# Conditioning rows at 0.7, 1.1, 1.1, 1.1 and 0.7 per block in five mixer projections, in place of 0.94 in all five

## Chip, cores and metric

The kernel runs on one core of a Trainium2 chip. The metric is the device time of one execution in microseconds, as the median of several runs. Before the change it is 2046.04 us (three runs, 2045.04 to 2049.21).

## The reference

One layer of a flow-matching trunk is applied to 128 context tokens and 256 latent tokens of width 2048. Both groups share the weights; each has its own conditioning vector, from which a matrix w_mod (2048 x 12288) makes six modulation vectors: sh1, sc1, g1 for the mixer and sh2, sc2, g2 for the feed-forward part.

```python
def _layer(x, mod, grid, s_ret0, c0, n0, m0, lp):
    sh1, sc1, g1, sh2, sc2, g2 = jnp.split(mod, 6, axis=-1)
    h = _ln(x) * (1.0 + sc1) + sh1
    mix, states = _mixer(h, grid, s_ret0, c0, n0, m0, w_in, b_gate, conv_qk, ret_theta,
                         gn_ret, gn_mlstm, w_out)
    x = _ln(ALPHA * x + g1 * mix) * ln1_g + ln1_b
    h = _ln(x) * (1.0 + sc2) + sh2
    x = _ln(ALPHA * x + g2 * _ffn(h, grid, w_up, conv_ff, w_down)) * ln2_g + ln2_b
    return x, states
# mod = silu(c) @ w_mod + b_mod, for the context's and the latents' vector
```

The mixer projects h with w_in (2048 x 8208), runs four heads of retention and four of mLSTM in both directions over the tokens, normalises each head, multiplies it by a gate and projects the result with w_out (2048 x 2048). The states of the context are outputs too.

## The kernel before

All 384 tokens are kept as 16 tiles of 128 features (kt = 0 to 15). Matrix products run in float32 split in two parts: ScalarE copies a weight tile to hi (L117), VectorE, and for one tile in six GpSimd, makes lo = raw - hi (L118), and TensorE adds three products, ah x hi, al x hi and ah x lo (L182 to L184 for products whose output has features on the partitions, tile psa; L190 to L192 for those with tokens on the partitions, tiles psb and pso).

**Mixer projections.** Heads are taken in a fixed order, four of retention and then four of mLSTM. The first two are projected in an earlier stage together with the first modulation vectors. A loop over i = 2 to 7 projects the other six. i = 2 and 3 are the last two of retention, i = 4 to 7 are the four of mLSTM, so the fourth projection is i=3 and the last is i=7. Each has 16 blocks, called steps here: 4 for q and 4 for k (psa, four kt in one weight tile, 24 matmuls) and 8 for v and gate (psb, two kt in one tile, 18 matmuls).

**What runs beside a step.** After each step, `beside()` gives one step to three generators: `mods2` (conditioning rows), `gating` (the gates of mLSTM) and `behind` (the attention of an earlier head). A Stepper collects its rate as credit and takes one item for each whole unit:

```python
        def step(self):
            self.credit += self.rate
            while self.gen is not None and self.credit >= 1.0:
                self.credit -= 1.0
                if next(self.gen, self) is self:
                    self.gen = None
```

Beside projection i runs the attention of head i-2; beside i=7 run those of heads 5 and 6, at rate 1.55. The attention of head 7, called attention(7), runs beside the first seven blocks of w_out, at rate 1.75, and is finished before the eighth.

**Conditioning rows.** `mod_vector` computes g1, sh2 and the first half of sc2 on VectorE, in five macc blocks of 16 rows. A row loads a tile mraw of 128 x 1024 of w_mod (512 KB, three buffers, loads two rows ahead, on SyncE's queue) and makes two VectorE instructions on macc, one for each conditioning vector (L283 for the first row of a block, L286 for the others). After 16 rows eight small matmuls with a matrix of ones sum macc over the partitions (L293, tile modr); VectorE adds the bias (L295) and GpSimd's queue writes the vector to DRAM (modrow). macc has one buffer, so the next block's first row can't start before this reduction has read the last one. The reduction of a block and the first row of the next are one item of the generator: the 17th, 33rd, 49th and 65th item, and the 81st ends it.

**Order.** The framework orders each engine's instructions before the program runs: an engine takes the instruction that stands first in the program among those that its own timing model holds ready. Work that stands later in the program can so be taken early where an engine would else be idle. On the chip each engine keeps that order.

**After the loop.** Attention(5) and (6) fill the last tiles of the mixer's output. The w_out product for the first 512 columns (tile pso) runs over kt 0 to 11, 14 and 15 in seven blocks, each followed by a step of `mods2` and of attention(7); kt 12 and 13 come from attention(7) and make the eighth block. The rest of w_out, the feed-forward part and the norms follow.

Of the kernel before, what the change touches and what calls it, by code (L numbers as in the profile page):

```python
# [82 lines left out]
def hybrid_step(ctx, tc, ca, cb, x_prompt, x_sample, state_ret, state_c, state_n, state_m, c, c_ctx,  # L83
# [51 lines left out]
    def rows_bcast(dst, src_row, n):  # L135
        nc.gpsimd.dma_start(out=dst, in_=src_row.to_broadcast([P, n]))
# [133 lines left out]
    def mod_vector(part, psp, mp, raws, js=range(2)):  # L270

        for j in js:
            col = part * D + j * 1024
            acc = mp.tile([P, 2, 1024], F32, tag="macc", name="macc", bufs=1)
            bt = mp.tile([P, 512], F32, tag="mbt", name="mbt", bufs=1)
            for hf in range(2):
                nc.gpsimd.dma_start(out=bt[64 * hf:64 * hf + 64, :],
                                    in_=b_mod[:, col + hf * 512:col + (hf + 1) * 512].to_broadcast([64, 512]))
            for kt in range(KT):
                raw = next(raws)  # L280
                for v in range(2):
                    if kt == 0:
                        nc.vector.tensor_scalar(out=acc[:, v, :], in0=raw, scalar1=ct[:, kt, v:v + 1],  # L283
                                                scalar2=None, op0=ALU.mult)
                    else:
                        nc.vector.scalar_tensor_tensor(out=acc[:, v, :], in0=raw, scalar=ct[:, kt, v:v + 1],  # L286
                                                       in1=acc[:, v, :], op0=ALU.mult, op1=ALU.add)
                yield
            ps = psp.tile([P, 512], F32, tag="ps", name="modr")
            for hf in range(2):  # L290
                for v in range(2):
                    g = 2 * hf + v
                    nc.tensor.matmul(ps[32 * g:32 * g + 32, :], lhsT=ones, rhs=acc[:, v, hf * 512:(hf + 1) * 512],  # L293
                                     start=True, stop=True)
            nc.vector.tensor_tensor(bt, ps, bt, op=ALU.add)  # L295
            for hf in range(2):
                for v in range(2):
                    g = 2 * hf + v
                    nc.gpsimd.dma_start(out=modrow[part, v:v + 1, j * 1024 + hf * 512:j * 1024 + (hf + 1) * 512],
                                        in_=bt[32 * g:32 * g + 1, :])  # L300
# [18 lines left out]
    def chain(*gens):  # L319
        for g in gens:  # L320
            yield from g
# [192 lines left out]
    with p1:  # L514
# [72 lines left out]
        def gates():  # L587
# [49 lines left out]
            for n, src in enumerate((ga, gem)):  # L637
                for d in range(2):
                    for tt in range(NT):
# [8 lines left out]
        mods2 = Stepper(chain(mod_vector(2, pat, mp, raws2), mod_vector(3, pat, mp, raws2),  # L648
                              mod_vector(4, pat, mp, raws2, range(NV))), 0.9)
# [257 lines left out]
        def attention(i):  # L907
            return heads[i][1](heads[i][2], *got[i])

        def new_acts(*kts):  # L910
            for kt in kts:
                new_act(kt, mixt[kt])

        for i in range(2, 8):
            mods2.rate = 0.0 if i == 2 else 0.94
            gating.rate = 0.6 if i == 3 else 0.0
            if i == 6:
                gating.finish()
                gn_m.append(tab.tile([P, 1024], F32, tag="gn", name="gnm"))
                rows_bcast(gn_m[0], gn_mlstm.rearrange("a h v -> a (h v)"), 1024)  # L920
            last = i == 7
            behind[:] = [Stepper(chain(*[attention(j) for j in ((5, 6) if last else (i - 2,))]), 1.55 if last else 1.0)]
            got.append(heads[i][0](heads[i][2], [lambda j=j: new_acts(2 * j, 2 * j + 1) for j in range(5)] if last else ()))
            behind.pop().finish()
        new_acts(10, 11, 14, 15)
        wo = w_out[0]
        pso = [pmm.tile([P, 512], F32, tag="ps", name="pso") for _ in range(NT)]
        attn = Stepper(attention(7), 1.75)
        attn.step()
        for k0 in (0, 2, 4, 6, 8, 10, 14):  # L930
            part_b(pso, weights_b(wo, k0, 2, (0,)), 2, k0, 0, 13)
# [55 lines left out]
    with ExitStack() as p2:  # L987
# [130 lines left out]
        for kt in range(KT):  # L1118
            if kt % 4 == 0:
                for ug in range(2):  # L1120
# [4 lines left out]
                    i = kt // 2 + ug  # L1125
# [238 lines left out]
```

## Time and profile before

| what | value |
|---|---|
| median of three runs | 2046.04 us (2045.04 to 2049.21) |
| profiled execution | 2043.59 us, of which the program's span is 2041.8 us |
| TensorE (PE) busy | 1982.6 us, 97% of the span |
| VectorE (DVE) busy | 1244.4 us, 61% |
| projections i = 2 to 7 | 228.5 to 733.5 us from the span's start |
| first 512 columns of w_out up to the eighth block | 733.5 to 799 us |

PE is TensorE's matmuls, PEld its weight loads, DVE VectorE, ACT ScalarE, POOL GpSimd, SP SyncE. Lines such as L286 are lines of the kernel. In the rows of instructions, "out<-in" names tiles, "x32" counts instructions, and a bracket gives the idle time of the engine before the first of them and what ended it. Busy matmuls are modelled from their starts, so PE can be called busy where it is not at its peak.

### The profile page before, as it was taken

To read this page: it belongs to the slowest core of one execution; us is meant where nothing else is said; L and a number is where in the kernel's file an instruction comes from. 1 tells how busy PE (TensorE), PEld (TensorE's weight loads), DVE (VectorE), ACT (ScalarE), POOL (GpSimd) and SP (SyncE) were. 2 spreads that over 40 slices of the span, in tenths; PEclk is the share of its full clock that TensorE was granted. 3 is DMA by queue.
4 is the path that set the end of the run, shared out by engine and by line. 5 is a ranking of instruction groups with operands and counts; after the bars stand their busy time and mean duration, and the time that the engine had idled before them with its cause. 6 is when DMAs were issued, how large, how long until landed. Compare 5 with 4: busy or idle time off the path is not lost.

```text
span 2041.8 us, 26592 instructions
## 1 busy us (share of the span) xinstructions
PE 1982.6 (97%) x10333; PEld 1747.4 (86%) x10333; DVE 1244.4 (61%) x1805; ACT 707.9 (35%) x1082; POOL 237.8 (12%) x233
## 2 busy tenths in 40 slices
PE   6899998999999998999999999999999999999997
PEld 4677888798898886678999889999889998999976
DVE  4555795487969894476964333449534445544478
ACT  4223334333343543236333333333222332333341
POOL 0001332231222222024000000000000000000003
PEclk9899999999999999998999999999999999999999
DMA  9895679587768765834764334447434444534342
GB/s 342 253 310 184 183 193 155 118 221 206 231 211 208 186 203 178 310 102 117 236 198 126 124 124 124 125 124 245 142 124 124 124 124 165 165 114 135 121 142 88
DMA packets 260638, 352.32 MB, mean 173 GB/s; under 512 B 16143, under 2 KB 200784, under 8 KB 259360
## 3 DMA queue, kind: packets, MB, share of 16 engines
q1 hardware_dynamic: 256240, 340.08, 55.6%
q0 software_dynamic: 4272, 10.54, 1.5%
q8 instruction: 81, 1.33, 0.3%
q14 instruction: 45, 0.37, 0.1%
HBM read 343.16 MB, written 7.41 MB: 172 GB/s over the span
## 4 chain that ended last, share of the span: by engine, by line
PE 84%; DVE 7%; issue 3%; DMA 3%; POOL 1%; SPq 1%; ACT 1%; DVEq 0%; POOLq 0%; ACTq 0%
PE psu L182 12%; PE psu L184 12%; PE psu L183 12%; PE psd L192 5%; PE psd L191 5%; PE psd L190 5%; PE psa L182 4%; PE psa L184 4%; PE psa L183 4%; PE psb L190 3%; PE psb L191 3%; PE psb L192 3%; DVE macc L286 3%; PE modps L255 2%; DMA mraw<-in_w_mod 2%
## 5 line engine op out<-in xcount | busy, mean ns | idle before, releaser
L118 DVE TENSOR_TENSOR lo<-raw,hi 128x1024 fp32r<-128x1024 f32 (+4 forms) x446 | 485.1, 1095 | 535.3 <-ACT hi L117 534.6
L117 ACT CAST hi<-raw 128x1024 fp32r<-128x1024 f32 (+4 forms) x476 | 438.0, 930 | 966.5 <-PE psu L183 358.5
L183 PE MATMUL psu<-al,hi 128*128 128x384 f32 (+1 forms) x1336 | 450.6, 338 | 0.0
L182 PE MATMUL psu<-ah,hi 128*128 128x384 f32 (+1 forms) x1336 | 448.9, 338 | 0.0
L184 PE MATMUL psu<-ah,lo 128*128 128x384 f32 (+1 forms) x1336 | 447.1, 338 | 0.0
L286 DVE SCALAR_TENSOR_TENSOR macc<-mraw,ct,macc 128x1024 f32<-128x1024 f32 x210 | 287.9, 1397 | 15.3 <-DMA mraw<-in_w_mod 15.1
L182 PEld LDWEIGHTS psu<-ah,hi 128*128 128x128 f32 x1336 | 249.5, 188 | 1.8 <-issue 0.8
L183 PEld LDWEIGHTS psu<-al,hi 128*128 128x128 f32 x1336 | 250.7, 188 | 0.1
L184 PEld LDWEIGHTS psu<-ah,lo 128*128 128x128 f32 x1336 | 250.5, 188 | 0.1
L191 PE MATMUL psd<-lo,fah 128*128 128x512 f32 (+1 forms) x496 | 194.9, 393 | 2.4 <-DVE lo L118 2.4
L192 PE MATMUL psd<-hi,fal 128*128 128x512 f32 (+1 forms) x496 | 196.6, 396 | 0.0
L190 PE MATMUL psd<-hi,fah 128*128 128x512 f32 (+1 forms) x496 | 189.7, 391 | 0.0
L184 PE MATMUL psa<-ah,lo 128*128 128x384 f32 x512 | 175.3, 344 | 7.0 <-DVE lo L118 6.9
L182 PE MATMUL psa<-ah,hi 128*128 128x384 f32 x512 | 179.5, 355 | 1.7 <-ACT hi L117 1.7
L183 PE MATMUL psa<-al,hi 128*128 128x384 f32 x512 | 175.3, 343 | 0.0
L191 PE MATMUL psb<-lo,ah 128*128 128x512 f32 x384 | 153.8, 401 | 0.5 <-DVE lo L118 0.5
L192 PE MATMUL psb<-hi,al 128*128 128x512 f32 x384 | 152.5, 397 | 0.0
L190 PE MATMUL psb<-hi,ah 128*128 128x512 f32 x384 | 149.9, 405 | 0.7 <-ACT hi L117 0.7
L191 PEld LDWEIGHTS psd<-lo,fah 128*128 128x128 f32 x496 | 93.1, 188 | 27.3 <-DVE lo L118 4.0
L182 PEld LDWEIGHTS psa<-ah,hi 128*128 128x128 f32 x512 | 96.6, 190 | 17.7 <-issue 11.6
L190 PEld LDWEIGHTS psd<-hi,fah 128*128 128x128 f32 x496 | 93.1, 188 | 21.7 <-ACT hi L117 0.2
L192 PEld LDWEIGHTS psd<-hi,fal 128*128 128x128 f32 x496 | 93.1, 188 | 21.3
(329 smaller groups left out, 2343.2 us busy)
## 6 DMA issues: line engine op xcount, KB each, us to landing
raw<-in_w_up SPq DMA_DIRECT2D x168, 512.0 KB, 3.8
mraw<-in_w_mod SPq DMA_DIRECT2D x112, 512.0 KB, 4.9
raw<-in_w_down SPq DMA_DIRECT2D x84, 512.0 KB, 3.6
raw<-in_w_in SPq DMA_DIRECT2D x128, 256.0 KB, 4.6
raw<-in_w_in SPq DMA_DIRECT2D x52, 512.0 KB, 7.1
wm<-in_w_mod SPq DMA_DIRECT2D x20, 1024.0 KB, 8.9
raw<-in_w_out SPq DMA_DIRECT2D x32, 512.0 KB, 4.7
wm<-in_w_mod SPq DMA_DIRECT2D x16, 768.0 KB, 6.1
```

The lines of the kernel that those rows point to most:

```text
L117: mark["hi"] = nc.scalar.copy(dst_hi, src).ins
L118: mark["lo"] = (eng or nc.vector).tensor_tensor(out=dst_lo, in0=src, in1=dst_hi.bitcast(F32), op=ALU.subtract).ins
L182: nc.tensor.matmul(ps, lhsT=hi[:, s], rhs=ah, start=start, stop=False)
L183: nc.tensor.matmul(ps, lhsT=hi[:, s], rhs=al, start=False, stop=False)
L184: nc.tensor.matmul(ps, lhsT=lo[:, s], rhs=ah, start=False, stop=stop)
L190: nc.tensor.matmul(ps, lhsT=ah[:, t], rhs=hi[:, s], start=start, stop=False)
L191: nc.tensor.matmul(ps, lhsT=ah[:, t], rhs=lo[:, s], start=False, stop=False)
L192: mark["mm"] = nc.tensor.matmul(ps, lhsT=al[:, t], rhs=hi[:, s], start=False, stop=stop).ins
L255: nc.tensor.matmul(ps[32 * g:32 * g + 32, :w], lhsT=ct[:, kt, :], rhs=raw[:, kk * w:(kk + 1) * w], start=kt < 4, stop=kt >= 12)
L286: nc.vector.scalar_tensor_tensor(out=acc[:, v, :], in0=raw, scalar=ct[:, kt, v:v + 1], in1=acc[:, v, :], op0=ALU.mult, op1=ALU.add)
```

## The change

In the loop over projections the rate of `mods2` is 0.7 for i=3 and i=7 and 1.1 for i = 4, 5 and 6, in place of 0.94 for all five. For i=2 it stays 0. After the loop the rate is set to 0.94, so that the steps beside w_out have the rate that they had. Nothing else is changed: rows, blocks, reductions, buffers and queues are the same.

```diff
         for i in range(2, 8):
-            mods2.rate = 0.0 if i == 2 else 0.94
+            mods2.rate = (0.0, 0.7, 1.1, 1.1, 1.1, 0.7)[i - 2]
             gating.rate = 0.6 if i == 3 else 0.0
...
         pso = [pmm.tile([P, 512], F32, tag="ps", name="pso") for _ in range(NT)]
         attn = Stepper(attention(7), 1.75)
+        mods2.rate = 0.94
         attn.step()
         for k0 in (0, 2, 4, 6, 8, 10, 14):
             part_b(pso, weights_b(wo, k0, 2, (0,)), 2, k0, 0, 13)
             mods2.step()
```

## The prediction

> **What bounds the kernel now.** The page comes first. In it TensorE (PE) is busy almost throughout, so a change to VectorE (DVE) work can pay only where PE waits for it.
>
> ```profile
> span 2041.8 us, 26592 instructions
> PE 1982.6 (97%) x10333; PEld 1747.4 (86%) x10333; DVE 1244.4 (61%) x1805; ACT 707.9 (35%) x1082; POOL 237.8 (12%) x233
> L286 DVE SCALAR_TENSOR_TENSOR macc<-mraw,ct,macc 128x1024 f32<-128x1024 f32 x210 | 287.9, 1397 | 15.3 <-DMA mraw<-in_w_mod 15.1
> ```
>
> A conditioning row is two DVE instructions on macc, 2 x 1.397 = 2.8 us by that group. Second view: busy time by stage, cut where the projection loop goes from one i to the next (i=2, 3, 5, 6 and 7 shown). The columns are the bounds, the length, busy time with instruction counts, the granted clock and the DMA.
>
> ```profile
> core 0: us, PE busy (x) PEld busy (x) DVE busy (x) ACT busy (x) POOL busy (x), PEclk, DMA share, GB/s
> 228.50:313.00 84.50, 80.45 (x393) 71.51 (x392) 78.87 (x96) 27.93 (x51) 34.28 (x28) 0.98 0.75 205
> 313.00:403.60 90.60, 85.65 (x418) 72.82 (x417) 49.09 (x78) 32.96 (x57) 19.89 (x19) 0.98 0.70 131
> 483.70:563.00 79.30, 79.30 (x400) 70.42 (x399) 65.64 (x77) 27.86 (x40) 18.08 (x18) 1.00 0.67 210
> 563.00:644.00 81.00, 81.00 (x400) 70.52 (x399) 63.61 (x103) 32.63 (x55) 17.29 (x17) 1.00 0.71 203
> 644.00:733.50 89.50, 88.15 (x434) 74.99 (x433) 80.00 (x126) 43.87 (x81) 24.52 (x20) 1.00 0.75 197
> ```
>
> Both stages that lose rows are some 10 us longer than their neighbours, but i=7 mostly because it carries two heads' attention (434 matmuls against 400). PE idles 5.0 us in i=3 and 1.4 us in i=7. Third view: the waits of PE in those two stages, and what DVE did before the first.
>
> ```profile
> PE psa L184 <- DVE lo L118: 5.0, 1, 5.0
> PE psa L184 <- DVE lo L118: 1.3, 1, 1.3
> 312.02 4.07 DVE L286 SCALAR_TENSOR_TENSOR macc<-mraw,ct,macc 128x1024 f32<-128x1024 f32 x2 [3.27 <-DMA mraw<-in_w_mod]
> 316.01 4.10 DVE L118 TENSOR_TENSOR lo<-raw,hi 128x512 fp32r<-128x512 f32 x4
> ```
>
> The 5.0 us stand at the start of i=3: a row's data landed late, and the split that PE needed stood behind it on DVE.
>
> The larger loss lies after the projections, in the part of w_out where the last head's attention ends. Fourth view: PE from the seventh w_out step on, and two of its waits.
>
> ```profile
> 761.60:777.00 15.40, 14.08 (x64) 10.80 (x64) 10.32 (x32) 8.53 (x17) 4.61 (x4) 1.00 0.47 151
> 777.00:799.00 22.00, 15.47 (x59) 9.98 (x58) 12.13 (x41) 8.56 (x23) 3.59 (x4) 0.87 0.30 100
> 781.10 0.70 PE L794 MATMUL num<-vx,wt 128*128 128x257 f32 x2 [2.58 <-DVE wt L762]
> 796.14 1.13 PE L114 MATMUL mxp<-cst,hh 128*128 128x128 f32 x6 [3.08 <-DVE hh L713]
> ```
>
> PE is idle 1.32 + 6.53 = 7.85 us there: its w_out blocks are used up at 777, and it follows the serial chain of head attention(7). That chain starts late because the one before it ended late. Fifth view: DVE from scores to the transposed output for attention(5), (6) and (7), first all of it, then macc alone.
>
> ```profile
> 650.30:696.80 46.50, 37.83 (x73) 1.00 0.79 179
> 699.48:769.70 70.22, 69.12 (x104) 1.00 0.64 211
> 769.78:797.20 27.42, 14.57 (x49) 0.93 0.31 106
> 650.30:696.80 46.50, 15.14 (x11) 1.00 0.79 179
> 699.48:769.70 70.22, 36.30 (x26) 1.00 0.64 211
> 769.78:797.20 27.42, 0.00 (x0) 0.93 0.31 106
> ```
>
> With no macc beside it such a head takes 27.4 us, with 11 macc 46.5, with 26 macc 70.2, and there DVE is busy 98%. So attention(6) is bound by DVE, half of it by conditioning rows.
>
> **The change part by part.** It adds and removes no instruction: both versions hand out 75 rows in i=3 to 7 (16 x 0.94 x 5 = 75.2 and 16 x (0.7 + 3 x 1.1 + 0.7) = 75.2), and w_out starts from the same credit at 0.94 again. What moves is where in the program each row and each block's reduction stands. 16 rows fill one macc (a single buffer); a reduction (L293, on PE) ends a block and frees macc for the next. Engines' orders are planned from program order, with later work pulled ahead into idle time. Sixth view: macc in the stretches of blocks (x32) and the breaks between (PE x8 is the reduction that ends a break).
>
> ```profile
> 316.20:420.40 104.20, 1.07 (x8) 0.16 (x8) 0.00 (x0) 0.98 0.67 131
> 420.40:482.30 61.90, 0.00 (x0) 0.00 (x0) 43.57 (x32) 1.00 0.86 239
> 503.90:569.10 65.20, 0.00 (x0) 0.00 (x0) 42.87 (x32) 1.00 0.73 239
> 569.10:593.20 24.10, 1.06 (x8) 0.16 (x8) 0.00 (x0) 1.00 0.47 142
> 593.20:661.00 67.80, 0.00 (x0) 0.00 (x0) 44.87 (x32) 1.00 0.85 221
> 661.00:690.10 29.10, 1.06 (x8) 0.16 (x8) 0.00 (x0) 1.00 0.79 172
> 690.10:761.60 71.50, 0.00 (x0) 0.00 (x0) 45.07 (x32) 1.00 0.64 204
> ```
>
> *i=3, rate 0.94 to 0.7: nothing, 0 us.* The first break covers it: block 1 is over at 316, three microseconds into i=3, so all its rows were pulled into i=2, where the rate is 0. They stay behind all work of i=2 and the first steps of i=3 in either version, so I expect the same order and the same 5.0 us stall. Bounds: 0, and a gain of 5.0 us if row 16, which hereafter belongs to step 5 of i=4 instead of step 2, no longer gets ahead of the split.
>
> *i=4 to 6, rate 1.1: reductions move.* Counting credit, the 17th call comes at step 6 of i=4 (11.2 + 6 x 1.1) instead of step 3, the 33rd at step 4 of i=5 in both, the 49th at step 3 of i=6 (46.4 + 3.3) instead of 5, the 65th at step 2 of i=7 (64.0 + 1.4) instead of 6. A projection step is 24 psa matmuls in its first half; seventh view, psa in windows that hold 6, 3 and 2 such steps, and the reduction as it is now.
>
> ```profile
> 403.58:437.90 34.32, 26.79 (x144) 1.00 0.70 172
> 562.90:578.30 15.40, 13.35 (x73) 1.00 0.72 248
> 643.90:657.80 13.90, 9.72 (x48) 1.00 1.00 255
> 688.40:689.60 1.20, 1.06 (x8) 0.16 (x8) 1.00 0.12 44
> ```
>
> So block 2 runs from about 439 to 501 (its 61.9 us), just before block 3 begins at 503.9, which stays; block 4 runs from about 580 to 648 (67.8 us) instead of 593 to 661; block 5 may start at about 659 instead of 690. In i=5 and i=6 the rates put 16 x 0.16 = 2.6 more rows each (7.2 us) into 13.7 and 17.4 us of idle DVE (79.30 - 65.64, 81.00 - 63.61). I cost this at 0; the cover is that idle time and the splits that lie ready for PE. If it is gone, PE stalls on lo as at 313: 0 to 5.0 us for each stall, and I take 0, since block 2 to 4 each ran in a DVE that was nearly full and i=5 and 6 show PE busy to the last hundredth. The moved reductions issue their bias and modrow DMAs on POOL's queue with them; the rows' loads move on SP's queue and are issued when a macc row frees one of three mraw buffers, so they follow the blocks.
>
> *i=7, rate 0.7, and the earlier fourth reduction.* Here the gain comes from. Eighth view: DVE in the present break, and the macc of block 4 in i=7.
>
> ```profile
> 661.00:690.00 29.00, 29.00 (x155) 26.15 (x154) 20.33 (x58) 14.44 (x30) 5.05 (x7) 1.00 0.79 171
> 647.65 4.07 DVE L286 SCALAR_TENSOR_TENSOR macc<-mraw,ct,macc 128x1024 f32<-128x1024 f32 x2 [0.83 <-DMA mraw<-in_w_mod]
> 652.78 4.60 DVE L286 SCALAR_TENSOR_TENSOR macc<-mraw,ct,macc 128x1024 f32<-128x1024 f32 x2
> ```
>
> In the break DVE has 29.0 - 20.3 = 8.7 us idle that block 5 could not use and now can. Besides, 8.7 us of block 4's macc leave i=7 for i=6. After the break, attention(6) competed with 16 rows that were overdue; at 0.7 a row, fewer stand ahead of it in the program. So attention(6) should end earlier by 0 (if rows only change places with its own work) to 17.4 us; I take 8.7, the idle time alone, since the other 8.7 us fall where macc is not yet free. Attention(7), 27.4 us long, then starts at 761 and ends at 788.5 instead of 797.2, beside the last two w_out blocks. PE can take back at most the 7.85 us it idles. I take 8: the gain is -8, between 0 and -10.
>
> At 796 to 799 PE also runs at a lowered clock after the 3.08 us wait; the reduction there is the row at half speed.
>
> ```profile
> 797.20 1.94 PE L293 MATMUL modr<-macc,ones 128*32 128x512 f32 x8
> ```
>
> It takes 1.94 us against 1.06 at full clock. I leave that as it is: the wait for hh ends the chain in either version. [...]
>
> *The sum.* 0 (i=3) + 0 (i=4 to 6) - 8 (end of attention) = -8 us. The profiled execution took 2043.59 us (span 2041.8, 1.8 around it), so 2035.6 by it. It lies 2.45 us under the median of 2046.04; taken to the median, 2038.
>
> **The rivals.** First, nothing happens: the rows are low in priority already, attention(6) is slowed by its own 104 - 26 other instructions and by the splits, and ends where it did. For it: in i=3 exactly that holds. Against it: 26 macc and 36.3 us of its 70.2. It gives 2046, within 4 us.
>
> Second, slower: rows 76 to 80 still stand in w_out at 0.94, and if attention(6) ends early they fall into attention(7), which has no macc now. Its chain is serial; 10 macc ahead of its links would cost 10 x 1.4 = 14 us. It decides once more than 6 macc (8.7 / 1.4) stand there. For it: 26 macc stretched attention(6). Against it: with block 5 begun 31 us sooner, its last row, now at 761, should be done at 740 to 750. If all ten fell there and attention(6) gained half (4 us), the time is 2046 - 4 + 14 = 2056.
>
> Third, the stall of i=3 goes as well: 8 + 5 = 13 us, 2033.
>
> **How the numbers follow.** The forecast, some 5 to 11 us faster, has 0.62, the third rival 0.06, no difference 0.21, slower 0.11. A difference under 0.2% (4.1 us) is about what can't be told from no change here, the three runs alone spread over 4.2 us. Faster 0.68, same 0.21, slower 0.11. The range goes from 2033 (third rival) to 2048, which takes in half of the no-difference case; outside are the slower rival and some of the ends.
>
> **What would show it.** Right: in i=3 two macc at 312 and a PE wait of 5.0 us as before; reductions near 438, 503, 579 and 658; macc nearly without a break from 659; attention(6) over by about 760; PE idle after 761 down from 7.85 us to some 2. Wrong: reduction 4 still near 688, or PE waiting on macc for it; new PE waits on lo in i=5 to 7; macc among attention(7)'s instructions; i=3 shortened, in which case pulling ahead doesn't work as I read it.

## The result, and the profile after

The changed kernel takes 2059.81 us (median of four runs, 2058.97 to 2062.19), the kernel before 2045.54 us beside it (four runs, 2042.94 to 2049.21). The ratio is 1.0075, 95% interval 1.0063 to 1.0086: slower by 14 us, where 8 us less was forecast and 2033 to 2048 given as the range.

The page of the changed kernel, and its stages i=3, 6 and 7 and the first part of w_out (bounds, length, busy time with instruction counts by engine, granted clock, DMA share, GB/s):

```profile
span 2060.4 us, 26584 instructions
PE 1988.6 (97%) x10333; PEld 1750.3 (85%) x10333; DVE 1245.9 (60%) x1805; ACT 704.4 (34%) x1079; POOL 236.6 (11%) x233
```

```profile
core 0: us, PE busy (x) PEld busy (x) DVE busy (x) ACT busy (x) POOL busy (x), PEclk, DMA share, GB/s
313.70:404.20 90.50, 85.67 (x417) 72.92 (x416) 49.05 (x78) 32.86 (x57) 19.83 (x19) 0.98 0.70 132
564.40:649.40 85.00, 82.99 (x400) 71.67 (x400) 70.81 (x101) 32.53 (x55) 18.00 (x16) 0.98 0.78 221
649.40:739.80 90.40, 85.95 (x407) 73.24 (x406) 84.87 (x125) 36.73 (x63) 22.27 (x16) 0.96 0.77 201
739.80:770.00 30.20, 30.20 (x133) 23.54 (x132) 14.58 (x30) 16.06 (x29) 6.99 (x6) 1.00 0.34 114
770.00:796.00 26.00, 21.39 (x85) 16.57 (x84) 12.04 (x41) 8.28 (x24) 3.92 (x7) 0.87 0.25 81
796.00:818.00 22.00, 15.47 (x59) 10.27 (x59) 12.58 (x42) 8.47 (x23) 3.79 (x5) 0.84 0.31 102
```

The same work is done (PE has as many matmuls, DVE as many instructions), and i=3 is as long as it was. i=6 takes 85.0 us instead of 81.0. DVE is nearly full in i=7, and half empty from 739.8 on; PE idles in i=6 and i=7 (2.0 and 4.5 us), and again from 770 on (11.1 us to 818).

The two profiled spans lie 18.6 us apart, more than the 14.3 of the medians: the profiled execution of before is 2.0 us under its median, that of after 2.4 above. Where the 18.6 us arise is read from three marks. The loop's i=6 begins at 564.44 (before 562.87), i=7 at 649.38 (643.88), the eighth w_out block at 817.68 (799.10). From that block to the end of the span both executions take 1242.7 us (2060.4 - 817.7, 2041.8 - 799.1). So 1.6 us come ahead of i=6, 3.9 from i=6, and 13.1 from i=7 and the seven w_out blocks. PE in these two stretches, without other engines; two rows of before, then two of after:

```profile
562.87:643.88 81.01, 81.01 (x399) 1.00 0.71 203
643.88:799.10 155.22, 146.02 (x678) 0.98 0.64 182
```

```profile
564.44:649.38 84.94, 82.93 (x400) 0.98 0.78 221
649.38:817.68 168.30, 152.71 (x678) 0.94 0.56 154
```

Length less busy time is PE's idle time: 9.2 us before and 15.6 after in the long stretch, 6.4 more. The other 6.7 of the 13.1 us are busy time: the same 678 matmuls took longer at a lower granted clock (0.94 against 0.98). In i=6 it is the same: 2.0 us idle and 1.9 more busy. PE's waits there, first i=6, then the long stretch:

```profile
PE psb L191 <- DVE lo L118: 2.0, 1, 2.0
```

```profile
PE mxp L114 <- DVE hh L713: 6.1, 2, 3.1
PE psb L191 <- DVE lo L118: 3.5, 1, 3.5
```

The prediction's view of DVE from a head's scores to its transposed output, now for attention(5), (6) and (7); first all of DVE, then macc alone:

```profile
660.42:749.21 88.79, 79.89 (x119) 0.96 0.71 195
749.32:785.67 36.35, 18.99 (x53) 0.97 0.35 116
785.88:815.43 29.55, 14.64 (x49) 0.85 0.21 72
660.42:749.21 88.79, 43.26 (x32) 0.96 0.71 195
749.32:785.67 36.35, 0.00 (x0) 0.97 0.35 116
785.88:815.43 29.55, 0.00 (x0) 0.85 0.21 72
```

All 32 macc of block 5 now stand beside attention(5), which takes 88.8 us instead of 46.5. Attention(6) is quick, as forecast (36.4 instead of 70.2), but begins 50 us later and ends 16 us later than before. After 749 there is no macc left, and two serial chains follow each other on a DVE that is half idle. How a row gets between the links of a chain, and how the new stall of i=7 arises (DVE, then PE; a bracket gives the idle time before, and what ended it):

```profile
687.16 5.42 DVE L286 SCALAR_TENSOR_TENSOR macc<-mraw,ct,macc 128x1024 f32<-128x1024 f32 x2
...
693.10 1.27 DVE L286 SCALAR_TENSOR_TENSOR macc<-mraw,ct,macc 128x1024 f32<-128x1024 f32 x1
...
694.94 1.27 DVE L286 SCALAR_TENSOR_TENSOR macc<-mraw,ct,macc 128x1024 f32<-128x1024 f32 x1
696.13 1.21 DVE L118 TENSOR_TENSOR lo<-raw,hi 128x1024 fp32r<-128x1024 f32 x1
...
707.35 0.14 DVE L797 TENSOR_TENSOR dn<-dn,gcol 128x1 f32<-128x1 f32 x1
707.42 1.27 DVE L286 SCALAR_TENSOR_TENSOR macc<-mraw,ct,macc 128x1024 f32<-128x1024 f32 x1
708.62 0.15 DVE L798 RECIPROCAL dn<-dn 128x1 f32<-128x1 f32 x1
```

```profile
697.40 0.50 PE L191 MATMUL psb<-lo,ah 128*128 128x512 f32 x1 [3.53 <-DVE lo L118]
```

Two links of the normaliser, 0.14 and 0.15 us long, have a macc of 1.27 us between them. Four macc stand in the 9 us ahead of the split at 696.13 (5.42 us for two of them, where two take 2.47 at 670.47; what stands beside them is in the last section), and PE waits 3.53 us for that split, whose hi was ready at 691.1.

### The profile page after: what moved, and what is told of

Same layout as the page of the kernel before. It is cut to its first block, busy times and chain, and to the rows that moved or that the text cites. A ratio compares the mean times of both kernels' runs of the same rounds, so it can differ in the third digit from the quotient of the medians.

```text
span 2060.4 us, 26584 instructions
## 1 busy us (share of the span) xinstructions
PE 1988.6 (97%) x10333; PEld 1750.3 (85%) x10333; DVE 1245.9 (60%) x1805; ACT 704.4 (34%) x1079; POOL 236.6 (11%) x233
## 4 chain that ended last, share of the span: by engine, by line
PE 82%; DVE 8%; DMA 4%; issue 3%; SPq 1%; POOL 1%; ACT 1%; DVEq 0%; POOLq 0%; ACTq 0%
PE psu L183 11%; PE psu L184 11%; PE psu L182 11%; PE psd L192 5%; PE psd L191 5%; PE psd L190 5%; PE psa L182 3%; PE psb L191 3%; PE psb L190 3%; PE psb L192 3%; DVE macc L286 3%; PE psa L184 3%; PE psa L183 3%; DMA mraw<-in_w_mod 2%; PE pso L190 2%
```

## The experiments

Each was measured beside the kernel before; the medians of before were 2044.76, 2044.46, 2044.02 and 2043.85 us in the four groups (e1, e2, e4, e5; e3, e6, e7, e8; e9, e10; e11, e12). Edits are against the kernel before unless said otherwise.

**e1_hold: the new rates up to i=6, the fourth reduction left at step 6 of i=7.** In `beside()` (against the changed kernel):

```diff
-            mods2.step()
+            if hold[0]:
+                hold[0] -= 1
+            else:
+                mods2.step()
...
-            mods2.rate = (0.0, 0.7, 1.1, 1.1, 1.1, 0.7)[i - 2]
+            mods2.rate = (0.0, 0.7, 1.1, 1.1, 1.1, 11.2 / 11)[i - 2]
+            hold[0] = 5 if i == 7 else 0
```

> Rates as in the changed kernel up to i=6 (64 rows handed out), but in i=7 no row before step 6, then 11.2/11 a step, so that the fourth reduction stands at step 6 as before the change. Theory A (the loss comes from block 5 starting at step 2 of i=7, which takes the macc-free stretch from attention(5)): most of the loss goes, 2045 to 2051 us; attention(5) again near 46 us. Theory B (the loss comes from the four more rows in i=6, which delay attention(4) and with it the chain of the last heads by 12 us): most of the loss stays, 2054 to 2060 us.

Measured: 2052.69 us, ratio 1.0035 (1.0022 to 1.0048), 7.9 us over before. macc beside attention(5) and (6):

```profile
659.60:706.70 47.10, 3.94 (x5) 1.00 0.66 145
709.20:777.00 67.80, 37.41 (x27) 0.99 0.63 209
```

The two heads take what they took before (47.1 and 67.8 against 46.5 and 70.2). What is left is the part ahead: i=7 starts 4.6 us later (648.5 against 643.9), and attention(4) ends at 659.8 instead of 648.3. The time lies between the ranges of the two theories: each has a part. Of the 7.9 us, 4.0 arise in i=6 (563.5 to 648.5 here) and 3.3 from i=7 to the eighth block (648.5 to 807.0).

**e2_last: the reverse, the old rates up to i=6 and the fourth reduction at step 2 of i=7, then 0.7 a step.**

```diff
-            mods2.rate = 0.0 if i == 2 else 0.94
+            mods2.rate = (0.0, 0.94, 0.94, 0.94, 0.94, 0.7)[i - 2]
+            mods2.credit += 3.84 if i == 7 else 0.0
```

> Rates as before the change up to i=6 (60 rows), but in i=7 the credit is raised by 3.84 at the start and the rate is 0.7, so that the fourth reduction is handed out at step 2 as in the changed kernel. Theory A: most of the loss is there, 2052 to 2060 us, attention(5) over 70 us. Theory B: little of it, 2044 to 2051 us, since attention(4) ends as before the change, near 648.

Measured: 2059.87 us, ratio 1.0072 (1.0055 to 1.0089), 15.1 us over before. macc beside attention(5), and the reduction:

```profile
651.20:747.50 96.30, 53.60 (x37) 0.96 0.76 208
660.91 3.03 PE L293 MATMUL modr<-macc,ones 128*32 128x512 f32 x8 [2.80 <-DVE macc L286]
```

The earlier fourth reduction alone gives the whole loss. Here it even stops PE for 2.8 us: its last macc was not yet done. The two parts don't add: 7.9 + 15.1 = 23 against 14 for both together.

**e4_after_no5 and e5_before_no5: block 5's sums left out, in the changed kernel and in the kernel before.** In `mod_vector`:

```diff
             for kt in range(KT):
                 raw = next(raws)
                 for v in range(2):
+                    if part == 4 and kt > 0:
+                        continue
```

> The changed kernel with block 5's sums left out but for its first row (its loads and its reduction stay; the first half of sc2 is wrong by that). Theories A and B agree that macc beside the attention of the last heads stretches their chain; A: without it the changed kernel has almost no loss left beside the one of the kernel before with the same cut, both at 2032 to 2040 us, within 4 us of each other. B: it stays 8 to 12 us behind that kernel, since attention(4) still ends late.

> The kernel before with block 5's sums left out but for its first row. Both theories: attention(6) falls from 70 us to 30 to 45 us, PE idles less after 761 us, and the time is 2034 to 2039 us (7 to 11 us less). If the time stays at 2043 to 2047 us, macc is not what stretches the chain.

Measured: 2045.23 us (e4) and 2038.36 (e5, ratio 0.9966, 0.9954 to 0.9977). Against before of its own group the changed kernel is at +14.3, e4 at +0.5 (ratio 1.0003, 0.9994 to 1.0013), e5 at -6.4. So block 5's sums cost 6.4 us before and 13.8 after: 7.4 of the 14.3 us are a higher price for the same 30 macc. The other 6.9 (e4 less e5) are there without them, and agree with e1's 7.9. The 6.9 lie between what theory A (within 4) and theory B (8 to 12) had expected, as in e1, and e4's time is above A's 2032 to 2040.

**e3_first: rates 0.7, 1.1, 1.02, 0.94, 0.94, the fourth reduction at step 6.**

```diff
-            mods2.rate = 0.0 if i == 2 else 0.94
+            mods2.rate = (0.0, 0.7, 1.1, 1.02, 0.94, 0.94)[i - 2]
```

> Only the first two of the five rates changed for good: 0.7, 1.1, 1.02, 0.94, 0.94, so that 45.12 rows are out at the end of i=5 and all is as before from i=6 on. Theory C (only the order of macc against the attention of heads 4 to 7 counts, which is one serial chain up to the eighth w_out block): no difference that can be told, 2043 to 2048 us. Rival D (back-to-back macc blocks cost PE time wherever they stand): i=4 longer by 2 us as in the changed kernel and the rest later by that or more, 2048 to 2052 us.

Measured: 2045.19 us, ratio 1.0004 (0.9995 to 1.0013). Nothing: the change in i=3, 4 and 5 alone is free, and attention(5) to (7) are as before (46.6, 70.1 and 27.5 us). With e1, the part ahead of i=7 that costs is the 1.1 in i=6 (85.0 us long in e1 too).

**e8_thin: as before up to step 6 of i=7, then 0.35 a step, the rest at 1.78 beside w_out.** A counter set at i=7 changes the rate from step 7 on:

```diff
+                if late7[0] == 10:
+                    mods2.rate = 0.35
...
+        mods2.rate = 1.78
```

> As before the change up to step 6 of i=7, where the fourth reduction stands; then only 0.35 rows a step in i=7 and 1.78 in w_out. Theory C with rows pulled ahead into idle time: what paces the rows of a block is DVE's idle time, not the rate; attention(6) still has over 20 macc beside it and the time is 2042 to 2048 us. Rival E (a lower rate puts attention(6) ahead of the rows in the order, as I had predicted): attention(6) ends 5 us or more earlier and the time is 2036 to 2041 us.

Measured: 2044.81 us, ratio 1.0 (0.9991 to 1.0009). macc beside attention(6), with a third of the rate:

```profile
699.50:769.70 70.20, 37.04 (x26) 1.00 0.66 215
```

It is the row of before (70.22 us, 26 macc). Handing rows out more thinly did not take them from beside attention(6): they are pulled ahead from where they stand, as the rows of block 1 are at 312. Here the place of the reduction, which frees macc, set when block 5 ran, and the rate behind it did nothing.

**e6_early, e7_from2, e9_burst: macc taken out of i=7**, by rates that finish the rows about its start or earlier.

```diff
-            mods2.rate = 0.0 if i == 2 else 0.94
+            mods2.rate = (0.0, 2.0, 1.0, 1.0, 1.0, 1.0)[i - 2]        # e6
+            mods2.rate = 1.0                                           # e7, i=2 too
+            mods2.rate = 0.0 if i == 2 else 1.3                        # e9
+            mods2.credit += 16.0 if i == 3 else 0.0                    # e9
```

> Rates 0, 2.0, 1.0, 1.0, 1.0, 1.0: 32 rows are out at the end of i=3, 80 at the end of i=6, and the first reduction moves from i=4 to step 9 of i=3, where DVE has 41 us idle. Theory C: no macc beside attention(5), (6) and (7); attention(4) still has some 30 to 40; the chain ends as in the kernel before with block 5's sums left out or a little earlier, 2033 to 2040 us. Rival D: DVE is full from i=3 to i=6 without a break, PE stalls on lo there, and it is 2044 us or more.

> Rate 1.0 in all six projections, i=2 too: the first reduction moves to step 1 of i=3, and 80 rows are out at the end of i=6. Theory C: as with 2.0 in i=3, but attention(4) has fewer macc beside it, since each block starts earlier; 2031 to 2039 us; rows 1 to 16 were in i=2 anyway. Rival D: 2044 us or more, by stalls in i=2 and i=3.

> Rate 0 in i=2, 16 rows of credit at the start of i=3 and 1.3 a step from there: reductions at step 1 and 14 of i=3, 10 of i=4, 6 of i=5 and 2 of i=6, so all macc is done by about 575 us and none stands beside the attention of heads 4 to 7 but for the first part of 4. Theory A: the end of the chain is as hidden as PE's own work allows; PE gains up to 10 us there and loses 4 to 8 us by waits on lo in i=3 to i=5, where DVE is full without a break; 2036 to 2044 us. Rival D (DVE without breaks costs more than that): 2046 us or more.

Measured: 2060.38 us (e6, ratio 1.0078, 1.0064 to 1.0091), 2048.91 (e7, 1.0021, 1.0012 to 1.003) and 2055.55 (e9, 1.0061, 1.0048 to 1.0074). PE from the start of i=2 to that of i=7, before and then in e7, and in e7 from there to the eighth block:

```profile
228.52:643.88 415.36, 406.36 (x2005) 0.99 0.73 193
```

```profile
228.51:657.11 428.60, 413.61 (x2017) 0.99 0.78 212
657.10:801.80 144.70, 141.15 (x669) 0.99 0.48 121
```

The last stretch is 10.5 us shorter than before (144.7 against 155.2), but i=7 begins at 657.1 instead of 643.9. PE idles 15.0 us ahead of it against 9.0. The other two begin i=7 at 670.0 and 669.1. All three miss the gain that theory C or A had expected of them and fit rival D's times. PE's waits for splits from i=2 to i=6 in e9 (13.3 us together in e6):

```profile
PE psa L184 <- DVE lo L118: 11.3, 3, 5.0
PE psb L191 <- DVE lo L118: 4.8, 4, 2.5
```

Before, these two were 5.0 and 0.5 us. With macc earlier and closer together the splits are late more often. That it is DVE's fullness alone is not shown: the longest new wait in e9 (4.8 us, at 606.5) follows 3.54 us in which DVE waited for a row's data.

**e11_step4, e12_step8 and e10_later: the fourth reduction at step 4, 8 and 10 of i=7** (before: 6; e2: 2), nothing changed ahead of i=7.

```diff
+            mods2.credit += 1.88 if i == 7 else 0.0                    # e11
...
+            if not 6 <= n7[0] <= 7:        # e12; e10: 6 to 9. No row in these steps,
+                ...                        # then 10.34 / 9 (e10: 10.34 / 7) a step
                 mods2.step()
```

> Before's rates with 1.88 more credit at the start of i=7: the fourth reduction is the item of step 4 of i=7 instead of step 6, nothing before i=7 changes. Theory (the place of the fourth reduction splits block 5 between attention(5) and attention(6)): some 18 to 22 macc beside attention(5), which takes 62 to 72 us instead of 46.8, and some 12 beside attention(6), which takes 50 instead of 70.1; attention(6) ends within 4 us of before's 769.5 and the time is within 5 us of before's. Rival (any reduction ahead of step 6 gives what step 2 gives): attention(5) over 85 us, no macc beside attention(6), some 2058.

> Before's rates, but in i=7 the conditioning rows rest in steps 6 and 7; the fourth reduction is the item of step 8, and the rest follow at 10.34/9 a step, 0.94 again in w_out. Theory (place of the fourth reduction): attention(5) about 45 us with 4 to 8 macc, attention(6) 72 to 80 with 26 to 30 macc, the time 2 to 10 us over before's, between step 6 (0) and step 10 (+13). Rival (a smooth optimum at step 6 is not there, the two steps only shift block 5 within attention(6)): within 2 us of before's.

> As before the change, but the rows rest from step 6 to 9 of i=7, so that the fourth reduction stands at step 10 in place of 6 (rate 10.34/7 from there). Theory A (the break's place counts): attention(5) keeps its macc-free stretch, attention(6) begins without macc and gets it from about 715, attention(7) gets the last rows; the loss of 15 us at step 2 does not go on as a gain, 2041 to 2049 us. If an earlier reduction costs and a later one pays in proportion (4 steps for 15 us), it would be under 2038 us.

Measured: 2048.90 (e11, ratio 1.0026, 1.0016 to 1.0036), 2050.09 (e12, 1.0033, 1.0021 to 1.0046) and 2056.89 (e10, 1.0062, 1.0047 to 1.0078). By the step of the reduction the time over before is 15.1 at 2, 5.1 at 4, 0 at 6, 6.2 at 8 and 12.9 at 10. macc beside attention(5) and (6) in e11, then e12, then e10:

```profile
649.50:735.10 85.60, 43.83 (x33) 1.00 0.82 226
735.00:774.10 39.10, 6.08 (x5) 0.96 0.36 123
```

```profile
651.40:696.40 45.00, 8.32 (x6) 1.00 0.81 182
700.90:775.20 74.30, 39.15 (x30) 0.97 0.63 209
```

```profile
651.70:695.70 44.00, 8.51 (x5) 1.00 0.77 171
699.70:783.80 84.10, 42.89 (x32) 0.94 0.58 189
```

The later side is as thought: 26, 30 and 32 macc beside attention(6) at steps 6, 8 and 10, which takes 70, 74 and 84 us. At step 10 its last links come after the w_out blocks are used up, and PE waits once 6.7 us for a dn product; the 2041 to 2049 us that theory A had expected there were missed. On the early side my account was only half right. At step 4 nearly all of block 5 is beside attention(5) too (33 macc of 43.8 us, 85.6 us long), not split as I had expected, yet that costs 5.1 and not 15.1 us. What step 2 has besides, in e2 and in the changed kernel alike, is PE stopped within i=7 (2.8 us for macc and 2.5 us for wt in e2, 3.5 us for lo in the changed kernel), each with a lowered clock after it (0.57 at 660 to 664 and 0.75 at 696 to 700 in e2, 0.50 at 700 to 704 in the changed kernel). e11 has no such stop, and the granted clock stays at 1.00 beside attention(5). The stop near 697 in the changed kernel follows two macc that were slow (5.42 us for both, where 1.27 is usual for one), but one of 3.32 us at 750.17 in the kernel before stops nothing (PE is busy without a gap from 746 to 762). Why those stops come at step 2 and not at 4 is open; so is why the two parts of the change don't add.

No version that was run with all its sums beats the kernel before.

## Why the prediction was wrong, point by point

**i=3: right.** Two macc at the same place and the same stall (4.8 us for lo against 5.0), and the stage is as long:

```profile
312.77 3.98 DVE L286 SCALAR_TENSOR_TENSOR macc<-mraw,ct,macc 128x1024 f32<-128x1024 f32 x2 [3.24 <-DMA mraw<-in_w_mod]
```

**Where the reductions go: right.** Forecast near 438, 503, 579 and 658; they stand at 435, 504, 582 and 665. The last macc ended at 738, forecast 740 to 750.

**"i=4 to 6, rate 1.1": costed at 0, measured at 7 to 8.** e1 gives 7.9, e4 against e5 6.9, and e3 puts it on i=6. There 34 macc instead of 29 stand beside attention(4), which takes 91.9 us instead of 81.2 and ends 12 us later (660.6 against 648.3), and PE has one wait on lo of 2.0 us. The cover that I named, idle DVE, was there in sum (85.0 - 70.8 = 14.2 us) but not where it was needed: DVE stands for 3.50 us ahead of a row whose data came late, and the split that PE needs, whose hi was ready at 637.5, comes behind that row.

```profile
638.75 1.28 DVE L286 SCALAR_TENSOR_TENSOR macc<-mraw,ct,macc 128x1024 f32<-128x1024 f32 x1 [3.50 <-DMA mraw<-in_w_mod]
...
641.55 1.20 DVE L118 TENSOR_TENSOR lo<-raw,hi 128x1024 fp32r<-128x1024 f32 x1
```

It is the stall of 312 in another place (3.24 us for the data there). I had put "0 to 5.0 us for each stall" and taken 0 because PE was busy to the last hundredth. That showed that nothing was late at the old rate, not how much room there was.

**"i=7, rate 0.7, and the earlier fourth reduction": the step that decided.** It was taken at -8 and bounded from 0 to 17.4 us of gain for attention(6), with no loss; e2 alone measures +15.1. Three things in it failed.

- I counted the break from 661 to 690 as 8.7 us of idle DVE for block 5 to fill. It was also the stretch in which attention(5) had its 46.5 us: a serial chain leaves DVE idle between links while other engines do theirs, and a macc started there makes the next link wait (1.27 us of macc at 707.42, ahead of a link of 0.15). With block 5 in it, attention(5) took 88.8 us. Its length alone does not set the time, though: 85.6 us of it cost 5.1 in e11, where PE had no new stop in i=7.
- I looked for the price at attention(7), the second rival, and found no macc there. That was so (0 macc). The head that paid was the one ahead, whose chain I had just shown as the quick one.
- I took PE's idle 7.85 us as the most at stake (the sum took 8 and its bound 10, both over it). New stalls lay in i=6 and i=7, where PE had idled 0 and 1.35 us, and the 7.85 themselves grew to 11.1 (from 770 on): PE waits there for hh of attention(6) too, some 3 us.

From i=7's start to the eighth block DVE now works less, and idles 20 us more (155.2 - 130.8 = 24.4 before, 168.3 - 123.8 = 44.5 after):

```profile
643.88:799.10 155.22, 130.77 (x234) 0.98 0.64 182
```

```profile
649.38:817.68 168.30, 123.77 (x236) 0.94 0.56 154
```

The macc taken early leave DVE nothing to do while attention(6) and (7) run one after the other. Idle time was moved, not filled.

**What would have told it.** My sign of a wrong forecast, "new PE waits on lo in i=5 to 7", came true (2.0 us in i=6, 3.5 in i=7). "No difference" fell too; the slower rival gave 2056, near the measured time, by a mechanism that did not occur.

## What to carry to other kernels

Idle time of an in-order engine is not free for low-priority work where a serial chain runs through it (here attention(5) went from 46.5 to 88.8 us): count the chain's links there, and what each waits when a longer instruction stands ahead, before calling it cover. Ask too whether the added work waits for a load, since what stands behind it then waits as well (in i=6 DVE stood 3.50 us for a row's data, and PE waited 2.01 us for the split behind that row). A break set by one buffer can be what lets the chain beside it run, so cost its filling as a loss first. When bulk work can't be removed, try its place from both sides: here each two steps of moving the release of macc off step 6, either way, cost 5 to 10 us.

## What of the hardware was not expected

A short stall of PE cost about twice its length here. In i=6 of the changed kernel PE waited 2.01 us, and the matmuls behind it ran slower for a while:

```profile
642.81 0.50 PE L191 MATMUL psb<-lo,ah 128*128 128x512 f32 x1 [2.01 <-DVE lo L118]
...
643.64 0.63 PE L191 MATMUL psb<-lo,ah 128*128 128x512 f32 x1
...
644.92 1.92 PE L810 MATMUL cst_ps<-vx,kw 128*128 128x257 f32 x4
...
647.04 0.40 PE L192 MATMUL psb<-hi,al 128*128 128x512 f32 x1
```

The slow stretch begins 0.8 us after PE resumed and lasts some 3.4 us (643.64 to 647.04). The granted clock was 0.51 in it, and 1.00 from 564.44 up to it and from its end to 649.38. By these two numbers it holds some 1.7 (3.4 x 0.49) of the 1.9 us of busy time that i=6 has more than before, beside the 2.0 of the wait. After the 3.53 us wait of i=7 the granted clock was 0.50 in one window of 4 us (700 to 704), with 0.77 and 0.87 in its neighbours:

```profile
696.00:700.00 4.00, 1.86 (x5) 0.77 0.62 191
700.00:704.00 4.00, 3.98 (x9) 0.50 0.58 177
704.00:708.00 4.00, 4.00 (x17) 0.87 0.22 67
```

How long a wait must be for this, and what sets the length of the slow stretch, no run shows. The prediction's sum had no term for a lowered clock; the added busy time was half of the loss from i=7 on (6.7 of 13.1 us).

A macc can be slow beside GpSimd. GpSimd was at work beside the two that took 5.42 us ahead of the stall of i=7:

```profile
686.87 2.40 POOL L118 TENSOR_TENSOR lo<-raw,hi 128x1024 fp32r<-128x1024 f32 x1 [9.69 <-ACT hi L117]
689.22 2.28 POOL L765 TENSOR_TENSOR qs<-q,sp 128x512 f32<-128x512 f32 x1
```

In this trace 155 of the kernel's 224 macc have no GpSimd instruction beside them, and the longest of these takes 1.29 us; 22 macc take over 1.5 us, and all of them have one beside them. The 47 others beside GpSimd are not slow (at most 1.29 us), and no run here took GpSimd's work away, so how much of the 3.53 us this made is open.
